# Sample attention's value products: every second key column, the sliding window and the new tokens as two tiles of 64 by 128 in place of four of 32 by 64

## The chip, the cores and the metric

The kernel runs on one core of a Trainium2 chip. The metric is the device time of one execution in microseconds (us). The engines of the core are TensorE (PE in the profile; its weight loads are PEld), VectorE (DVE), ScalarE (ACT), GpSimd (POOL) and SyncE (SP); the last two issue most of the data transfers. Each engine runs its own instructions in order and waits for the others by semaphores.

## The reference

One step of a decoder layer for a prompt of 512 tokens and for a sample group of 8 sequences with 8 new tokens each, on top of 2048 cached tokens a sequence. Only the sample group's attention matters here. Each sequence has two attention branches of 8 heads: "fox" (with forgetting) and "NSA" (three parts: selected blocks of keys, a sliding window of 512 keys, compressed keys). Both have 8 query heads, four to each of two key/value heads (groups) of 64 channels.

```python
def fox_attend(q, cq, q_pos, k, v, ck, k_pos):
    s = jnp.einsum('btgrd,bsgd->bgrts', q, k).astype(jnp.float32) * HEAD_DIM ** -0.5
    bias = jnp.moveaxis(cq, 1, -1)[..., :, None] - jnp.moveaxis(ck, 1, -1)[..., None, :]
    p = masked_softmax(s + bias, k_pos[None, :] <= q_pos[:, None])
    return jnp.einsum('bgrts,bsgd->btgrd', p.astype(v.dtype), v)

    # nsa_attend, its three products with values, g the group, r the head in it
    o_c = jnp.einsum('bgrtn,bngd->btgrd', p_c.astype(vc.dtype), vc)
    o_s = jnp.einsum('bgrtjs,bgtjsd->btgrd', p_s.astype(vsel.dtype), vsel)
    o_w = jnp.einsum('bgrtw,bwgd->btgrd', p_w.astype(vw.dtype), vw)
    return gates[..., 0:1] * o_c + gates[..., 1:2] * o_s + gates[..., 2:3] * o_w
```

For one sequence, one branch and one group there are 4 heads x 8 tokens = 32 query rows, and the values of that group have 64 channels. So a product with values is, for each group, weights (keys by 32) against values (keys by 64). Everything here is in f32.

## The kernel before

The sample attention is the method `sample_attention`. Its loop has a step for each of the 8 sequences `b`. The 2048 cached keys lie on 128 partitions in 16 columns `c` (`fr` for fox, `sr` for NSA; three such rooms are loaded in turn, `room` is the third), keys in the first 128 channels of a column, values in the last 128, both groups side by side. The 128 softmax rows are 2 branches x 2 groups x 32.

In a step, TensorE does the scores `ss` (`sequence_scores`, in four PSUM banks), the scores against the new tokens `sn`, then products with the values of the sequence before (`values(b - 1, ...)`). Meanwhile VectorE adds the biases into `S` (tile `zF`) and takes maxima, and ScalarE exponentiates in two halves. TensorE then transposes the weights (`turn_weights`: `spn`, then `sp` in four groups of four columns), ScalarE copies them to `T` (`spT` and `zK`), and TensorE does the first columns of `values(b, ...)` ahead of the next `ss`. The number of columns done where is: in even steps 12 of the sequence before and 8 of this one; in odd steps 8 and 4; the last sequence has its 16 at the end. Even steps also have the window's scores `sw`, odd steps the window's values (`window_values`, for two sequences at once) and `pair_sums` (`accS`), which picks out the results and adds them up. TensorE's instructions of the whole stage are chained in the order in which the code writes them (`link`); VectorE's and ScalarE's order is a scheduler's, within the bounds that `issue_after` sets.

The value products go into one PSUM bank, `so`. A key column is four products with 32 weight columns each (`quarters`):

```python
        for x in range(4):
            self.mm(self.sob[32 * x:32 * x + 32, col:col + 64], T[:, 32 * x:32 * x + 32],
                    values[x // 2][:, 64 * (x % 2):64 * (x % 2) + 64], start, stop)
```

Row quarter `x` of the bank belongs to branch `x // 2` and group `x % 2`. The new tokens' product (`TN`, 64 keys), the window's four columns (`TW`, 128 keys each), its new tokens (`TWn`) and the compressed keys (`pcT`, 127 keys) go the same way. `sequence_end` and `window_end` scale the results into `OA` and `OAw` on VectorE, and `sums` multiplies them by selection matrices into `accS`.

Of the kernel before, what the change touches and what calls it, by code (L numbers as in the profile page):

```python
# [6 lines left out]
F32 = mybir.dt.float32  # L7
# [4 lines left out]
OP = mybir.AluOpType  # L12
AX = mybir.AxisListType

P = 128
# [30 lines left out]
class Step:  # L46
# [55 lines left out]
    def ts(self, out, a, s1, s2, op0, op1=None, **kw):  # L102
        if op1 is None:
            self.last_ts = self.nc.vector.tensor_scalar(out, a, s1, s2, op0=op0, **kw).ins
        else:
            self.last_ts = self.nc.vector.tensor_scalar(out, a, s1, s2, op0=op0, op1=op1, **kw).ins
# [1513 lines left out]
    def sample_attention(self, sp, ctx):  # L1620

        t = lambda name, shape, dt=F32: sp.tile(shape, dt, name=name)
# [5 lines left out]
        self.T = [t(f"spT{i}", [P, 4, P]) for i in range(2)] + [  # L1628
            flat[1][:, 512 * i:512 * i + 512].rearrange("p (j n) -> p j n", j=4) for i in range(2)]
        self.sel, self.selW = [t(f"sel{g}", [P, 64]) for g in range(2)], [[t(f"selW{o}{g}", [P, 64]) for g in range(2)] for o in range(2)]  # L1630
        self.SN, self.OA, self.OAw = [[t(f"{n}{x}", [P, 64]) for x in range(2)] for n in ("sN", "OA", "OAw")]
        maps = [t(f"map{x}", [P, n]) for x, n in enumerate((2, 2, 2, 4))]
        pw = self.pool("spw", ctx)
        self.D3.append(pw.tile([P, 16, 32], F32, name="D3b"))
        pw.tile([P, 224], F32, name="edge")
        w1 = pw.tile([P, 4, 256], F32, name="wr1")
        self.CT = pw.tile([P, 512], F32R, name="CT")
        self.wrt = [pw.tile([P, 4, 256], F32, name="wr0"), w1]
# [26 lines left out]
        for b in range(NB):  # L1665
            n, odd = b // 2, b % 2
# [100 lines left out]
            self.cp(self.oT[:, 4 * a:4 * a + 4, SEQ:NT].rearrange("p r (b t) -> p r b t", t=8), av[:, a])  # L1767

    def pair_sums(self, n):
        w = self.OAw[n % 2]  # L1770
        for o in range(2):
            self.sums(2 * n + o, self.sel, self.OA[o], True)
            self.sums(2 * n + o, self.selW[o], w, False)

    def sample_maps(self, maps):

        jj = self.OA[0]
        self.iota(jj, [[1, 64]])
        col, up, gm, tmp = maps
        ts = self.ts  # L1780
        ts(up[:, 1:2], self.prow, 64.0, None, OP.is_ge)
        ts(up[:, 0:1], up[:, 1:2], -1.0, 1.0, OP.mult, OP.add)
        ts(col[:, 1:2], self.p31, 32.0, None, OP.add)
        self.stt(col[:, 0:1], up[:, 1:2], 32.0, self.p31, OP.mult, OP.add)
        self.cp(gm[:, 1:2], self.g_row)
        ts(gm[:, 0:1], self.g_row, -1.0, 1.0, OP.mult, OP.add)
        for g in range(2):
            ts(self.sel[g], jj, col[:, 0:1], gm[:, g:g + 1], OP.is_equal, OP.mult)
            for o in range(2):
                t = tmp[:, 2 * g + o:2 * g + o + 1]  # L1790
                self.tt(t, up[:, o:o + 1], gm[:, g:g + 1], OP.mult)
                ts(self.selW[o][g], jj, col[:, 1:2], t, OP.is_equal, OP.mult)
# [70 lines left out]
    def turn_weights(self, b):  # L1863
# [5 lines left out]
        for i in range(4):  # L1869
# [2 lines left out]
                self.tr(tb[:, P * j:P * j + P], self.S[:, 4 * i + j].rearrange("p q s -> p (q s)"))  # L1872
            self.last_weights = self.act(self.T[i], tb.rearrange("p (j n) -> p j n", j=4)).ins

    def quarters(self, col, T, values, start, stop):


        for x in range(4):
            self.mm(self.sob[32 * x:32 * x + 32, col:col + 64], T[:, 32 * x:32 * x + 32],
                    values[x // 2][:, 64 * (x % 2):64 * (x % 2) + 64], start, stop)  # L1880

    def values(self, b, part):
        col = 128 * (b % 2)
        fr, sr = self.rows[b]
        for i in part:
            T = self.T[i]
            for j in range(4):
                c = 4 * i + j
                self.quarters(col, T[:, j], (fr[:, c, P:256], sr[:, c, P:256]), c == 0, False)
        if part[-1] == 3:  # L1890
            self.quarters(col, self.TN, (self.vnew[:, 0, :], self.vnew[:, 1, :]), False, True)

    def sequence_end(self, b):

        mx, dn, nm = self.stat.pop(b)
        d = self.small.tile([P, 1], F32, tag="sd", name=f"sd{b}")
        self.nc.vector.tensor_reduce(d, dn, axis=AX.X, op=OP.add)
        self.nc.vector.reciprocal(d, d)
        col = 128 * (b % 2)
        self.ts(self.OA[b % 2], self.sob[:, col:col + 64], d, self.GA[:, b:b + 1], OP.mult, OP.mult)  # L1900
        self.last_end = self.last_ts

    def sums(self, b, sel, OA, first):

        for g in range(2):
            self.mm(self.acc[64 * g:64 * g + 64, 64 * b:64 * b + 64], OA, sel[g], first, not first)

    def window_keys(self, b):
        tb = self.trb(f"wk{b}")
# [33 lines left out]
        self.values(NB - 2, range(2, 4))  # L1943

    def window_values(self, i):
        col = 256 + 128 * (i % 2)
        wr = [self.wr.pop(2 * i + o) for o in range(2)]
        for j in range(4):
            self.quarters(col, self.TW[:, j], [w[:, j, P:256] for w in wr], j == 0, False)
        self.quarters(col, self.TWn, [self.vnew[:, 2, :]] * 2, False, True)  # L1950
        self.quarters(col + 64, self.pcT[:127, i], [self.vc[:127, 2 * i + o] for o in range(2)], True, True)

    def window_end(self, i):
        st, col = self.wst.pop(i), 256 + 128 * (i % 2)
        self.nc.vector.reciprocal(st[:, 3:4], st[:, 3:4])
        w = self.OAw[i % 2]
        self.ts(w, self.sob[:, col:col + 64], st[:, 3:4], self.GB[:, 1, i:i + 1], OP.mult, OP.mult)
        self.last_end = self.stt(w, self.sob[:, col + 64:col + 128], self.GB[:, 0, i:i + 1], w, OP.mult, OP.add).ins

    def mix_open(self):  # L1960

# [777 lines left out]
```

## Time and profile before

| | |
|---|---|
| median of 3 runs | 1146.51 us (1145.56 to 1148.76) |
| profiled execution | 1145.33 us, its span 1143.6 us |
| granted TensorE clock, mean | 0.992 |
| TensorE matmuls in the program | 9089 |
| matmuls into `so` | 1280, from 437.0 to 535.4 us |
| TensorE idle just before them, waiting for "issue" | 16.4 us, 18 times (loads and matmuls) |

A row of a timeline gives start, duration, engine, line, operation, tiles (out<-in) and shapes: "128*32 128x64" is a stationary operand of 128 partitions by 32 columns against a moving operand of 128 by 64. An f32 product is two matmul rows. Line 77 is the helper that all matmuls go through, so tiles tell them apart. A row of a stage has, in order, its length, the busy time (and instructions) of PE, PEld, DVE, ACT and POOL, the granted clock, the busy share of the transfer engines and GB/s. In the chain of waits, "issue" is time in which an engine waited for nothing that the profile shows.

### The profile page before, as it was taken

The numbers are of one execution on the slowest core, as the hardware profiler recorded it, in microseconds if no ns is written. First come the engines' busy times: TensorE is split into PE (matmuls) and PEld (weight loads), VectorE is DVE, ScalarE is ACT, GpSimd is POOL, SyncE is SP. The second block draws the span as 40 slices with busy tenths as digits, with TensorE's granted clock in tenths as the row PEclk, the third lists the DMA queues.
The fourth block names the chain that finished last, engine by engine and source line by source line (L and its number), as shares of the span: only waits on it lengthen the run. The fifth ranks groups of instructions, "written<-read, shape, count | busy, mean of one in ns | idle before, by whom it ended". The sixth has DMA issues, their size and how long they took to land.

```text
span 1143.6 us, 24614 instructions
## 1 busy us (share of the span) xinstructions
PE 1086.8 (95%) x9089; PEld 937.3 (82%) x9089; DVE 820.2 (72%) x2011; ACT 544.2 (48%) x1146; POOL 229.8 (20%) x319
## 2 busy tenths in 40 slices
PE   3999999999999997889999999999999999999998
PEld 3887789988666654556999999998988989899896
DVE  5988665675787867677977757669657657475668
ACT  3466653444777754457644434473413424143230
POOL 7540000001211414441000000012312122221202
PEclk9999999999999998999999999999999999999999
DMA  8998594764786799996543273351313224132132
GB/s 199 292 270 235 195 278 150 244 220 136 250 276 196 214 271 318 329 353 198 128 111 99 68 222 101 96 170 49 111 38 111 76 73 147 38 111 74 56 120 83
DMA packets 169049, 191.75 MB, mean 168 GB/s; under 512 B 17849, under 2 KB 147330, under 8 KB 166754
## 3 DMA queue, kind: packets, MB, share of 16 engines
q1 hardware_dynamic: 154818, 152.05, 44.8%
q0 software_dynamic: 11936, 37.10, 9.9%
q8 instruction: 71, 1.16, 0.4%
q10 hardware_dynamic: 2176, 1.05, 0.4%
q14 instruction: 48, 0.39, 0.1%
HBM read 179.89 MB, written 31.16 MB: 185 GB/s over the span
## 4 chain that ended last, share of the span: by engine, by line
PE 74%; DVE 10%; DMA 6%; ACT 4%; issue 3%; SPq 2%; POOL 1%; DVEq 0%; ACTq 0%; POOLq 0%
PE dn L77 16%; PE hid L77 5%; PE z L77 5%; PE br L77 4%; PE wo L77 4%; PE upv L77 3%; PE upx L77 3%; PE ss L77 3%; PE mg L77 2%; DMA winr<-in_w_in 2%; SPq L155 2%; PE so L77 2%; PE mgv L77 2%; PE mgx L77 2%; PE upz L77 2%
## 5 line engine op out<-in xcount | busy, mean ns | idle before, releaser
L100 DVE TENSOR_TENSOR acc<-acc,dn 128x512 f32<-128x512 f32 x66 | 44.5, 684 | 55.9 <-PE dn L77 55.9
L77 PE MATMUL hid<-xh,w1hlk 128*128 128x256 f32 (+1 forms) x192 | 46.7, 336 | 15.5 <-ACT xh L112 15.5
L77 PE MATMUL z<-winh,h2r 128*128 128x264 f32 (+1 forms) x288 | 57.3, 288 | 2.5 <-ACT adw L112 2.5
L77 PE MATMUL z<-winh,h 128*128 128x264 f32 (+1 forms) x288 | 55.9, 284 | 0.0
L112 ACT ACTIVATE xh<-cpg 128x512 fp32r<-128x512 f32 x64 | 37.4, 623 | 36.2 <-PE hid L77 20.5
L112 ACT ACTIVATE u<-c 128x512 fp32r<-128x512 f32 x64 | 24.1, 434 | 59.9 <-PE dn L77 45.3
L77 PE MATMUL hid<-xh,w1hlv 128*128 128x256 f32 (+1 forms) x192 | 48.1, 342 | 4.2 <-ACT w1hlv L112 2.9
L2403 POOL TENSOR_TENSOR wur<-wur 128x512 f32<-128x512 f32 x12 | 19.8, 1648 | 150.9 <-DVE wu1l L131 55.5
L131 DVE TENSOR_TENSOR xl<-cpg,xh 128x512 fp32r<-128x512 f32 x64 | 42.3, 682 | 10.1 <-ACT xh L112 10.1
L77 PEld LDWEIGHTS z<-winh,h2r 128*128 128x128 f32 x288 | 45.6, 190 | 3.8 <-ACT adw L112 2.7
L77 PEld LDWEIGHTS hid<-xh,w1hlk 128*128 128x128 f32 x192 | 32.6, 197 | 19.4 <-ACT xh L112 15.7
L77 PEld LDWEIGHTS z<-winh,h 128*128 128x128 f32 x288 | 45.8, 190 | 0.0
L470 DVE STREAM_TRANSPOSE cpg<-cpg 128x1024 f32<-128x1024 f32 (+1 forms) x36 | 39.2, 1109 | 8.8 <-DMA cpg<-in_cache_nsa_kv 8.8
L77 PE MATMUL z<-winl,h 128*128 128x264 f32 (+1 forms) x160 | 44.5, 284 | 0.5 <-DVE winl L131 0.5
L77 PE MATMUL z<-winl,h2r 128*128 128x264 f32 (+1 forms) x160 | 44.4, 284 | 0.0
L155 POOL DMA_DIRECT2D cpg<-in_cache_nsa_kv x72 | 37.7, 525 | 27.4 <-issue 13.7
L77 PEld LDWEIGHTS hid<-xh,w1hlv 128*128 128x128 f32 x192 | 33.7, 203 | 8.5 <-ACT w1hlv L112 3.1
L77 PE MATMUL br<-oL,wbh 128*128 128x288 f32 x128 | 37.7, 295 | 0.0
L77 PE MATMUL br<-oH,wbl 128*128 128x288 f32 x128 | 37.7, 294 | 0.0
L77 PE MATMUL br<-oH,wbh 128*128 128x288 f32 x128 | 37.7, 294 | 0.0
L1828 DVE CUSTOM_DVE_ANT_1 zF<-ss,scr 128x512 f32<-128x512 f32 x32 | 20.2, 687 | 20.2 <-PE ss L77 20.2
L131 DVE TENSOR_TENSOR winl<-winr,winh 128x1056 fp32r<-128x1056 f32 (+1 forms) x16 | 19.6, 1233 | 19.4 <-ACT winh L112 19.3
(926 smaller groups left out, 3604.3 us busy)
## 6 DMA issues: line engine op xcount, KB each, us to landing
adw<-in_w_ada SPq DMA_DIRECT2D x16, 1024.0 KB
foxD<-in_cache_fox_kv SPq DMA_DIRECT2D x128, 128.0 KB
wur<-in_w_up SPq DMA_DIRECT2D x32, 512.0 KB
wdr<-in_w_down SPq DMA_DIRECT2D x32, 512.0 KB
wada<-in_w_ada SPq DMA_DIRECT2D x8, 1024.0 KB
sr<-in_cache_nsa_kv SPq DMA_DIRECT2D x64, 128.0 KB
cpg<-in_cache_nsa_kv POOLq DMA_DIRECT2D x56, 128.0 KB, 6.0
cpg<-in_cache_nsa_kv SPq DMA_DIRECT2D x56, 128.0 KB
```

The costliest lines, as they stand in the source:

```text
L77: ins = self.nc.tensor.matmul(out, a, b, start=start, stop=stop, skip_group_check=True)
L100: self.nc.vector.tensor_tensor(out, a, b, op=op)
L112: return self.nc.scalar.activation(out, in_, f, **kw)
L131: self.splits.append((eng or self.nc.vector).tensor_tensor(l, x, h.bitcast(F32), op=OP.subtract).ins)
L155: self.issued[eng] = getattr(self.nc, eng).dma_start(out, in_).ins
L470: self.flipped = self.nc.vector.transpose(v, v).ins
L1828: self.nc.vector.tensor_tensor_reduce(self.S[:, :, q, :], pbs[q].rearrange("p (c s) -> p c s", s=32), self.ramp[:, None, 32 * (q % 2):32 * ...
L2403: gp(a12, a12, a11, op=OP.subtract)
```

## The change

`values` sends every second column (j even) and the new tokens to a new method `halves`, and so does `window_values` for all its products. A half is one branch: 64 weight columns (both groups) against the 128 value channels of both groups. Of the 64 by 128 result the two diagonal blocks of 32 by 64 (group with its own group) are wanted, the other two are not. Quarters now write their group's columns of the same 128, so that both kinds add into the same places; `OA` and `OAw` become 128 wide, and `sums` takes from them the 64 columns of its group. To make room, `OAw` has one buffer in place of two, the window has one set of 256 columns in place of two sets of 128, and an unused tile shrinks.

```diff
+    def halves(self, col, T, values, start, stop):
+
+        for o in range(2):
+            half = slice(64 * o, 64 * o + 64)
+            self.mm(self.sob[half, col:col + P], T[:, half], values[o], start, stop)
+
     def quarters(self, col, T, values, start, stop):
         for x in range(4):
-            self.mm(self.sob[32 * x:32 * x + 32, col:col + 64], T[:, 32 * x:32 * x + 32],
-                    values[x // 2][:, 64 * (x % 2):64 * (x % 2) + 64], start, stop)
+            c = 64 * (x % 2)
+            self.mm(self.sob[32 * x:32 * x + 32, col + c:col + c + 64], T[:, 32 * x:32 * x + 32], values[x // 2][:, c:c + 64], start, stop)
...
                 c = 4 * i + j
-                self.quarters(col, T[:, j], (fr[:, c, P:256], sr[:, c, P:256]), c == 0, False)
+                (self.quarters if j % 2 else self.halves)(col, T[:, j], (fr[:, c, P:256], sr[:, c, P:256]), c == 0, False)
         if part[-1] == 3:
-            self.quarters(col, self.TN, (self.vnew[:, 0, :], self.vnew[:, 1, :]), False, True)
+            self.halves(col, self.TN, (self.vnew[:, 0, :], self.vnew[:, 1, :]), False, True)
...
-        self.ts(self.OA[b % 2], self.sob[:, col:col + 64], d, self.GA[:, b:b + 1], OP.mult, OP.mult)
+        self.ts(self.OA[b % 2], self.sob[:, col:col + P], d, self.GA[:, b:b + 1], OP.mult, OP.mult)
...
         for g in range(2):
-            self.mm(self.acc[64 * g:64 * g + 64, 64 * b:64 * b + 64], OA, sel[g], first, not first)
+            self.mm(self.acc[64 * g:64 * g + 64, 64 * b:64 * b + 64], OA[:, 64 * g:64 * g + 64], sel[g], first, not first)
...
-        col = 256 + 128 * (i % 2)
+        col = 256
         wr = [self.wr.pop(2 * i + o) for o in range(2)]
         for j in range(4):
-            self.quarters(col, self.TW[:, j], [w[:, j, P:256] for w in wr], j == 0, False)
-        self.quarters(col, self.TWn, [self.vnew[:, 2, :]] * 2, False, True)
-        self.quarters(col + 64, self.pcT[:127, i], [self.vc[:127, 2 * i + o] for o in range(2)], True, True)
+            self.halves(col, self.TW[:, j], [w[:, j, P:256] for w in wr], j == 0, False)
+        self.halves(col, self.TWn, [self.vnew[:, 2, :]] * 2, False, True)
+        self.halves(col + P, self.pcT[:127, i], [self.vc[:127, 2 * i + o] for o in range(2)], True, True)
```

The order of the instructions shows it at three places. First TensorE, the last columns of the first block of sequence 0 (`so` from the weights `spT`) and the window's scores `sw` behind them, ahead of the next sequence's `ss`; before:

```order
L77 MATMUL so<-fr_6090,spT_6382 32x64 x2
L77 MATMUL so<-sr_5697,spT_6382 32x64 x2
L77 MATMUL sw_6711<-wkt_6408,bdN 64x512
L77 MATMUL sw_6711<-wkt_6409,bdN 64x512
L77 MATMUL ss_6737<-fr_6379,scr 32x512
```

and after, the last two columns:

```order
L77 MATMUL so<-fr_6090,spT_6382 64x128
L77 MATMUL so<-sr_5697,spT_6382 64x128
L77 MATMUL so<-fr_6090,spT_6382 32x64 x2
L77 MATMUL so<-sr_5697,spT_6382 32x64 x2
L77 MATMUL sw_6702<-wkt_6407,bdN 64x512
L77 MATMUL sw_6702<-wkt_6408,bdN 64x512
L77 MATMUL ss_6728<-fr_6379,scr 32x512
```

The product of a column with fox and NSA values is four instructions in a quarter column, two in a half column, and the two kinds alternate. Second TensorE, the end of a window's values (`wr` its cached values, `vnew` the new ones, `vc` the compressed ones) and the first sums; before:

```order
L77 MATMUL so<-wr_6406,scr 32x64 x2
L77 MATMUL so<-wr_6404,scr 32x64 x2
L77 MATMUL so<-vnew,TWn 32x64 x4
L77 MATMUL so<-vc,pers 32x64 x4
L77 MATMUL accS<-sel_6383,OA_6391 64x64
```

and after:

```order
L77 MATMUL so<-wr_6405,scr 64x128
L77 MATMUL so<-wr_6403,scr 64x128
L77 MATMUL so<-vnew,TWn 64x128 x2
L77 MATMUL so<-vc,pers 64x128 x2
L77 MATMUL accS<-sel_6383,OA_6391 64x64
```

Here all are halves, and the sums that follow are tiles of 64 columns too. Third VectorE in step 0, between the window's score biases and the biases of sequence 1 (`sel`, `selW` and `map` are the selection matrices made once, `sr` the keys of sequence 1); before:

```order
L106 TENSOR_SCALAR selW_6387<-OA_6391,map_6395,map_6398 128x64
L106 TENSOR_SCALAR selW_6385<-OA_6391,map_6395,map_6398 128x64
L100 TENSOR_TENSOR map_6398<-map_6396,map_6397 128x1
L106 TENSOR_SCALAR selW_6388<-OA_6391,map_6395,map_6398 128x64
L1955 RECIPROCAL swst_6595<-swst_6595 128x1
L1809 STREAM_TRANSPOSE sr_6380<-sr_6380 128x4x128
```

and after:

```order
L106 TENSOR_SCALAR selW_6387<-OA_6391,map_6394,map_6397 128x64
L1810 STREAM_TRANSPOSE sr_6380<-sr_6380 128x4x128
L106 TENSOR_SCALAR selW_6385<-OA_6391,map_6394,map_6397 128x64
L100 TENSOR_TENSOR map_6397<-map_6395,map_6396 128x1
L106 TENSOR_SCALAR selW_6388<-OA_6391,map_6394,map_6397 128x64
L1961 RECIPROCAL swst_6594<-swst_6594 128x1
```

The transpose of the last keys of sequence 1 stands four instructions earlier.

More of the change, by code (lines that the diff above doesn't have):

```diff
@@ L1630, in sample_attention @@
         self.sel, self.selW = [t(f"sel{g}", [P, 64]) for g in range(2)], [[t(f"selW{o}{g}", [P, 64]) for g in range(2)] for o in range(2)]
-        self.SN, self.OA, self.OAw = [[t(f"{n}{x}", [P, 64]) for x in range(2)] for n in ("sN", "OA", "OAw")]
+        self.SN = [t(f"sN{x}", [P, 64]) for x in range(2)]
+        self.OA, self.OAw = [t(f"OA{x}", [P, P]) for x in range(2)], t("OAw", [P, P])
         maps = [t(f"map{x}", [P, n]) for x, n in enumerate((2, 2, 2, 4))]
@@ L1634, in sample_attention @@
         self.D3.append(pw.tile([P, 16, 32], F32, name="D3b"))
-        pw.tile([P, 224], F32, name="edge")
+        pw.tile([P, 96], F32, name="edge")
         w1 = pw.tile([P, 4, 256], F32, name="wr1")
@@ L1769, in pair_sums @@
     def pair_sums(self, n):
-        w = self.OAw[n % 2]
+        w = self.OAw
         for o in range(2):
@@ L1775, in sample_maps @@
     def sample_maps(self, maps):
-        jj = self.OA[0]
+        jj = self.OA[0][:, 0:64]
         self.iota(jj, [[1, 64]])
@@ L1945, in window_values @@
     def window_values(self, i):
-        col = 256 + 128 * (i % 2)
+        col = 256
         wr = [self.wr.pop(2 * i + o) for o in range(2)]
         for j in range(4):
-            self.quarters(col, self.TW[:, j], [w[:, j, P:256] for w in wr], j == 0, False)
-        self.quarters(col, self.TWn, [self.vnew[:, 2, :]] * 2, False, True)
-        self.quarters(col + 64, self.pcT[:127, i], [self.vc[:127, 2 * i + o] for o in range(2)], True, True)
+            self.halves(col, self.TW[:, j], [w[:, j, P:256] for w in wr], j == 0, False)
+        self.halves(col, self.TWn, [self.vnew[:, 2, :]] * 2, False, True)
+        self.halves(col + P, self.pcT[:127, i], [self.vc[:127, 2 * i + o] for o in range(2)], True, True)
     def window_end(self, i):
-        st, col = self.wst.pop(i), 256 + 128 * (i % 2)
+        st, col = self.wst.pop(i), 256
         self.nc.vector.reciprocal(st[:, 3:4], st[:, 3:4])
-        w = self.OAw[i % 2]
-        self.ts(w, self.sob[:, col:col + 64], st[:, 3:4], self.GB[:, 1, i:i + 1], OP.mult, OP.mult)
-        self.last_end = self.stt(w, self.sob[:, col + 64:col + 128], self.GB[:, 0, i:i + 1], w, OP.mult, OP.add).ins
+        w = self.OAw
+        self.ts(w, self.sob[:, col:col + P], st[:, 3:4], self.GB[:, 1, i:i + 1], OP.mult, OP.mult)
+        self.last_end = self.stt(w, self.sob[:, col + P:col + 2 * P], self.GB[:, 0, i:i + 1], w, OP.mult, OP.add).ins
     def mix_open(self):
```

## The prediction

> **What bounds the kernel now.** I read the page first, then the stages, then the chain of waits and TensorE's rows where the changed tile `so` is written. The page and two stages:
>
> ```profile
> span 1143.6 us, 24614 instructions
> PE 1086.8 (95%) x9089; PEld 937.3 (82%) x9089; DVE 820.2 (72%) x2011; ACT 544.2 (48%) x1146; POOL 229.8 (20%) x319
> 437.00:536.00 99.00, 83.65 (x2027) 53.68 (x2027) 67.51 (x213) 51.33 (x113) 35.97 (x70) 0.97 0.88 298
> 536.00:740.00 204.00, 203.83 (x1595) 202.50 (x1594) 156.39 (x329) 96.55 (x176) 6.71 (x12) 1.00 0.42 120
> ```
>
> The change touches only 437 to 536 us, the eight sequences of the sample. There TensorE (first pair of numbers) idles 15 of 99 us; behind it TensorE is full (203.83 of 204.00), so a delay or gain at 536 us reaches the end undiminished. What the changed lines cost, and what TensorE waits for:
>
> ```profile
> L77 PE MATMUL so<-fr,spT x192: 216/219/317, 437.0 to 534.2; 128*32 128x64 f32 x192
> PE so L77 <- issue: 7.2, 6, 2.2
> PE sp L83 <- issue: 2.0, 1, 2.0
> PE ss L77 <- issue: 0.8, 1, 0.8
> ```
>
> The longest waits are "issue", 10.0 us, waits for nothing the profile shows. Where do they fall? Take one stage between two of them, and the queue that carries instructions over 425 to 545 us:
>
> ```profile
> 488.93:494.68 5.75, 4.98 (x128) 3.69 (x128) 5.75 (x13) 5.45 (x12) 4.01 (x8) 1.00 1.03 342
> q8 instruction: 17, 0.28, 0.9%
> ```
>
> 128 matmuls and 128 weight loads: 256 instructions between one wait's end and the next. Counted in the trace, all nine such waits end at instruction 193 of a block of 256. 0.28 MB in 17 packets is 16.5 KB each, and the page's 9089 + 9089 instructions over its 71 packets are 256 a packet. So these are waits for the next block of instructions, fetched while the DMA engines are full (share 1.03). Start to start the nine gaps sum to 12 us: a block was used up before the next arrived.
>
> **The change part by part.** On TensorE, of every four key columns two keep four tiles of 32 by 64 ("quarters") and two get two of 64 by 128 ("halves"), in turn. What each costs, from TensorE's rows in order of time:
>
> ```profile
> 459.04 0.23 PE L77 MATMUL so<-fr,zK 128*32 128x64 f32 x2
> ...
> 459.26 0.23 PE L77 MATMUL so<-fr,zK 128*32 128x64 f32 x2
> ...
> 461.77 0.25 PE L77 MATMUL so<-fr,zK 128*32 128x64 f32 x2 [2.24 <-issue]
> ...
> 461.85 0.22 PE L77 MATMUL so<-fr,zK 128*32 128x64 f32 x2
> ...
> 461.97 0.22 PE L77 MATMUL so<-fr,zK 128*32 128x64 f32 x1
> ...
> 462.13 0.32 PE L77 MATMUL so<-vnew,TN 64*32 64x64 f32 x8
> ```
>
> An f32 product is two passes; four tiles run side by side, and four passes take 459.26 - 459.04 = 0.22 us, 0.055 a pass, 0.11 a column. The first pass after a break takes 0.08 (461.77 to 461.85), its weight load being uncovered. Where the tile shape changes, the last pass takes 0.16 (461.97 to 462.13): the array runs empty first. Halves are not in this trace; their nearest rows are the two 64-column tiles of `accS` and a 128-wide transpose ahead of `so`:
>
> ```profile
> 478.49 0.32 PE L77 MATMUL so<-vc,pers 127*32 127x64 f32 x8
> 478.73 0.34 PE L77 MATMUL accS<-sel,OA 128*64 128x64 f32 x4
> 478.90 0.29 PE L77 MATMUL accS<-selW,OAw 128*64 128x64 f32 x4
> 479.02 0.29 PE L77 MATMUL accS<-sel,OA 128*64 128x64 f32 x4
> ...
> 447.12 0.30 PE L83 MATMUL spwn<-identF,scr 128*64 128x128 f32 x1
> 447.35 0.25 PE L77 MATMUL so<-fr,zK 128*32 128x64 f32 x2
> ```
>
> Two regular passes of 64 moving columns take 0.12 (478.90 to 479.02), the first two 0.17: 0.05 of load uncovered. 32 to 64 columns empties the array too: 0.24 from 478.49 to 478.73 for a first pass and a last (0.08 + 0.16). A pass of 128 moving columns takes 0.109 (16 transposes in 1.75 us, row 491.46 below), and one followed by another tile shape 0.23, of which 0.05 is load: 0.18 to 0.21.
>
> So a half column between two quarters costs 0.05 + 0.11 + 0.21 = 0.37, and a quarter column between two halves 0.08 + 0.16 = 0.24: **0.61 a pair, where a pair cost 0.22**. If the array did not empty between the two shapes, it would be 0.22 + 0.11 = 0.33. I take 0.61, since every change of shape in the rows above, both ways, shows the emptying. [...]
>
> A block of 12 columns thus gains 2.2 us, of 8 columns 1.4, of 4 columns 0.65, the last of 16 columns 3.0 (0.39 a pair, less the 0.1 by which the old block ended in a change anyway). The 8-row token product (`TN`) goes from 0.24 to 0.37, eight times. A window's four columns, all halves without a change between them, go from 0.5 to 1.0, its `TWn` gains 0.1; the compressed product is followed by `accS` in the same shape and gains nothing. In all 3 x 2.2 + 8 x 1.4 + 3 x 0.65 + 3.0 + 8 x 0.13 + 4 x 0.6 = **26 us more on TensorE**.
>
> Against it, 384 matmuls and 384 loads fewer in this stage, three blocks of 256. A block's time rises from about 6.5 us to 8 or 9, more than nearly all the fetch times seen (intervals of 5.6 to 8.4 us where TensorE waited). I let the nine waits go and keep 0.5 us.
>
> Neither sum lies wholly on the path. From the end of `ss` TensorE needs nothing for 5.75 us but has `so` of the sequence before to do, while VectorE and ScalarE make the softmax. An even step shows both parts:
>
> ```profile
> 481.98 3.82 PE ss L77 x67
> ...
> 487.53 0.69 PE so L77 x38
> 488.21 0.71 issue
> 488.93 1.30 PE so L77 x66
> 490.22 1.01 PE sw L77 x4
> ...
> 491.46 1.75 PE sp L83 x16
> 493.21 0.69 PE so L77 x40
> 493.90 0.77 issue
> 494.68 0.54 PE so L77 x24
> 495.22 3.40 PE ss L77 x68
> 490.42 1.13 ACT L112 ACTIVATE zF<-zF,ss 128x1024 f32<-128x1024 f32 x1
> ```
>
> The last row is ScalarE's: the second half's exponentials end at 491.55, 5.75 us after `ss` (485.80), and TensorE comes to `sp` at 491.46. There is no slack left: 12 columns and token, 2.0 now plus the wait of 0.7, become 4.1, and 8 columns, 1.2 plus 0.8, become 2.5: 1.9 us longer, less 0.3 that `ss` now waits at its start. Rows of an odd step (5), of the last, and of one stage inside step 2:
>
> ```profile
> 500.16 1.31 issue
> 501.47 2.13 PE so L77 x97
> ...
> 505.97 1.97 issue
> ...
> 521.41 3.34 PE ss L77 x63
> 524.75 0.82 issue
> ...
> 533.43 2.17 PE so L77 x136
> 464.00:465.00 1.00, 1.00 (x7) 1.00 (x6) 1.00 (x3) 0.92 (x2) 0.35 (x1) 0.50 1.08 354
> ```
>
> Step 5: 8 and 4 columns, token and window add 2.2; both waits (3.3) go: -1.1. Done so for each step, from one `ss` to the next: step 2, 3.6 more against its wait of 2.2 (2.24 above) and some 1.6 for the half clock that followed it (0.50 in the last row, while `sp` and `wk` ran): -0.2; step 3, +0.2; step 4, +1.6; step 5, -1.1; step 6 (no wait in it) 3.8 more, of which 1.3 fills waits for exponentials and for the next `ss`: +2.5; step 7, 16 columns at its open end (3.0), 1.4, 0.1 and 0.6 before it, less 0.8 of wait and 0.3 of cover: +4.0. Together +7.0. Step 0 has 8 columns ahead of a VectorE chain that sets the next `ss`: +1.2, less 0.6 since VectorE's transpose now stands ahead of three mask operations. Step 1: +0.9. With the 0.5 kept, **+9 us**.
>
> The wider normalisations on VectorE (16 or so by 64 elements, 0.07 us each) lie under TensorE's work; the loads that POOL issues when `so` frees a room come later by as much as TensorE does. The shared `OAw` and window columns are rewritten a whole step after their last reader.
>
> The profiled execution took 1145.3 us, 1.2 under the runs' median of 1146.5. On it the sum gives 1154.3, on the median 1155.5; I say 1155.
>
> **The rivals.** (1) *No emptying between the two column widths*, the one that makes it faster: 0.33 a pair. Then 12 columns are 2.0, inside the softmax's 5.75; steps fall to what VectorE and ScalarE need, and stage 437 to 536 ends 4.1 us earlier in steps 2 to 7, later by 0.7 in 0 and 1: 1143. For it: the tiles stand on the same columns and the rows at 128 partitions. Against: 478.49 to 478.73 is exactly this change, and it emptied. It decides at about 0.41 a pair (3.4 of the 12.4 us between the two cases, from 0.33). (2) *The issue waits stay*, moved to other blocks: the columns' cost without the gain. Without the waits the old steps 2 to 7 would end 5.1 us earlier, so 1155.5 + 5.1 = 1161. Against: fewer instructions in more time. [...] (3) *The softmax covers more*: the even steps' extra is hidden as step 2's, and only step 7's 4.0 less some of the waits is left: within 3 us, 1148.
>
> **How the numbers follow.** Forecast 0.62 (1151 to 1160 by itself: the drain at 0.18 or 0.21 and waits of 0 to 4 us left); rival 1, 0.12; rival 2, 0.13; rival 3, 0.13. A measurement of this kernel tells about 0.3%, 3.4 us. Faster: most of rival 1 and some of 3: 0.12. Same: 0.14. Slower: 0.74. The range leaves out a tenth at each end: 1145 to 1163.
>
> **What would show it.** Matmuls fall to 8705. Right: `so` rows of 64 columns with 0.2 us from a half's second pass to the next quarter and 0.16 back; "issue" below 3 us; the stage longer by 9 us, most in steps 4, 6 and 7. Wrong: a pair of columns at 0.33 (rival 1), or waits of 1 to 2 us still every 256 instructions (rival 2).

## The result, and the profile after

| | before | the change |
|---|---|---|
| median | 1147.44 us (7 runs) | 1155.25 us (7 runs) |
| ratio | | 1.0065, 95% interval 1.0036 to 1.0094 |
| the same once more, beside another set of runs of before | 1145.76 us (23 runs) | 1155.71 us (6 runs), 1.0102 (1.0073 to 1.0130) |
| profiled execution, its span | 1145.33, 1143.6 us | 1155.25, 1153.6 us |

The change makes the kernel slower, by 8 us in one set of runs and by 10 in the other; 9 was forecast (1155, range 1145 to 1163). The change's page (engines; the queue that carries instructions, with packets and MB):

```profile
span 1153.6 us, 23844 instructions
PE 1109.7 (96%) x8705; PEld 945.3 (82%) x8705; DVE 824.3 (71%) x2011; ACT 545.3 (47%) x1146; POOL 229.0 (20%) x319
q8 instruction: 68, 1.11, 0.4%
```

Two stages of it, the second taken 10 us later, since the sample's stage now ends about that much later:

```profile
437.00:536.00 99.00, 95.01 (x1499) 54.97 (x1495) 67.82 (x210) 48.35 (x108) 35.44 (x69) 0.98 0.86 289
546.00:750.00 204.00, 203.83 (x1590) 202.61 (x1590) 153.63 (x323) 91.19 (x165) 4.90 (x9) 1.00 0.39 111
```

TensorE has 384 matmuls fewer, the queue that carries instructions has 68 packets in place of 71, and TensorE is busy 22.9 us longer (19.1 in a second profile, see 1 below). In the sample's stage its idle time fell from 15 to 4 of 99 us; the stage behind it is as full as before. So the idle time was filled and more than filled. The view of TensorE's waits in this stage (what waited, for what: us, times, longest):

```profile
PE ss L77 <- DVE sr L1810: 2.0, 1, 2.0
PE so L77 <- ACT zK L112: 1.2, 1, 1.2
PE sn L77 <- ACT wkt L112: 0.5, 2, 0.3
...
```

No "issue" is left of the 10 us. A new wait of 1.2 us stands ahead of a product with values; it comes back below. One pair of columns in TensorE's rows by time: the last passes of a quarter column, a half column, a quarter column and the start of the next half.

```profile
458.31 0.23 PE L77 MATMUL so<-fr,spT 128*32 128x64 f32 x2
...
458.47 0.32 PE L77 MATMUL so<-fr,spT 128*64 128x128 f32 x1
...
458.63 0.27 PE L77 MATMUL so<-fr,spT 128*64 128x128 f32 x1
...
458.84 0.25 PE L77 MATMUL so<-fr,spT 128*32 128x64 f32 x2
...
458.92 0.23 PE L77 MATMUL so<-fr,spT 128*32 128x64 f32 x2
...
459.09 0.32 PE L77 MATMUL so<-fr,zK 128*64 128x128 f32 x1
```

From the first pass of a half (458.47) to that of the next (459.09) the pair takes 0.62 us: 0.16 from a quarter's last pass into the half, 0.16 for the half's first pass, 0.21 from its second into the quarter, 0.08 for the quarter's first. 0.61 was forecast.

Where the time went, from the start of one step's `ss` to the next (the last, to the first `mg`), in us. The last column is the change's second profile:

| step | before | the change | moved | forecast | the change again |
|---|---|---|---|---|---|
| 0 and 1 | 32.83 | 34.82 | +2.0 | +1.5 | 34.89 |
| 2 | 14.81 | 14.84 | 0.0 | -0.2 | 14.80 |
| 3 | 12.81 | 12.59 | -0.2 | +0.2 | 12.59 |
| 4 | 13.24 | 14.45 | +1.2 | +1.6 | 14.49 |
| 5 | 13.74 | 12.63 | -1.1 | -1.1 | 12.59 |
| 6 | 12.52 | 14.45 | +1.9 | +2.5 | 14.49 |
| 7 | 14.12 | 21.51 | +7.4 | +4.0 | 18.82 |

Step 7 alone is far off. The stage starts up to 8 us earlier or later from one profile to the next, whatever the kernel (first `ss` between 418 and 426 us); so below kernels are compared by these steps and by their timed ratios, not by spans. That the first profile took just the 1155 that was forecast is luck: its step 7 holds time that the forecast did not have (see 1).

### The profile page after: what moved, and what is told of

It is laid out like the page before. It is cut to its first block, busy times and chain, and to the rows that moved or that the text cites. A ratio compares the mean times of both kernels' runs of the same rounds, so it can differ in the third digit from the quotient of the medians.

```text
span 1153.6 us, 23844 instructions
## 1 busy us (share of the span) xinstructions
PE 1109.7 (96%) x8705; PEld 945.3 (82%) x8705; DVE 824.3 (71%) x2011; ACT 545.3 (47%) x1146; POOL 229.0 (20%) x319
## 4 chain that ended last, share of the span: by engine, by line
PE 81%; DMA 6%; DVE 5%; SPq 3%; ACT 2%; issue 2%; POOL 0%; ACTq 0%; POOLq 0%; DVEq 0%
PE dn L77 18%; PE z L77 9%; PE br L77 4%; PE wo L77 4%; PE so L77 4%; PE up L77 4%; PE upx L77 3%; PE upv L77 3%; DMA cpg<-in_cache_nsa_kv 3%; SPq L155 3%; PE ss L77 2%; PE mg L77 2%; PE hid L77 2%; PE mgv L77 2%; PE mgx L77 2%; PE upy L77 2%
## 5 line engine op out<-in xcount | busy, mean ns | idle before, releaser
L77 PE MATMUL hid<-xh,w1hlk 128*128 128x256 f32 (+1 forms) x192 | 46.6, 335 | 15.2 <-ACT xh L112 15.2
L131 DVE TENSOR_TENSOR xl<-cpg,xh 128x512 fp32r<-128x512 f32 x64 | 42.3, 683 | 10.2 <-ACT xh L112 10.1
L112 ACT ACTIVATE wu1h<-wur 128x512 fp32r<-128x512 f32 (+1 forms) x21 | 13.5, 651 | 40.9 <-PE upv L77 24.6
```

What stands on the lines that cost most here:

```text
L77: ins = self.nc.tensor.matmul(out, a, b, start=start, stop=stop, skip_group_check=True)
L112: return self.nc.scalar.activation(out, in_, f, **kw)
L131: self.splits.append((eng or self.nc.vector).tensor_tensor(l, x, h.bitcast(F32), op=OP.subtract).ins)
```

## Experiments

The ratio stands beside the median of the runs of before that were made with it: 1145.22 us (first four), 1145.76 (the change again, split halves, left out, light loads), 1146.03 (to the fifth, behind, behind with window), 1144.53 (the last). Apart from the change each kernel has one profile; those of left out, light loads and behind are of the longest execution of their kernel, so a wait that stands there need not be in the median.

**1. The change once more.** No edit.

> The change once more, unaltered, to see whether the 10 us of half TensorE clock at the end of its stage (537.5 to 547.7 us in its profile) belong to it. Theory (they follow from the wait of 1.2 us for ScalarE there): they are in this profile too, and the time is 1155. Rival (they fall by the history of the execution, as the dips of 3 us elsewhere do): step 7 takes some 17 us in place of 21.5 and the profiled execution 1151.

Measured: 1155.71 us, ratio 1.0102 (1.0073 to 1.0130); the profiled execution took 1151.35 us. The same stretch of both as a stage, the first profile of the change, then this one:

```profile
537.00:547.50 10.50, 10.50 (x110) 6.72 (x109) 6.21 (x10) 6.46 (x12) 1.80 (x3) 0.52 0.77 245
```

```profile
537.00:547.50 10.50, 10.50 (x147) 8.25 (x142) 9.07 (x14) 7.84 (x14) 1.80 (x3) 1.00 0.79 270
```

The granted clock is the third number from the right: 0.52 against 1.00. In the first profile 110 matmuls went through in this time, in the second 147. Step 7 falls from 21.51 to 18.82 us, and the 16 `mg` products behind it from 3.72 to 2.33. So about 4 us of the first profile are a half clock that this change does not need to have; the rival was right. Steps 0 to 6 agree within 0.1 us in both profiles. The second profile is of the shortest of its six executions.

**2. Halves grouped.** Halves in the first two of each four columns, quarters in the last two: the same instructions, half the changes of shape.

```diff
-                (self.quarters if j % 2 else self.halves)(col, T[:, j], ...
+                (self.quarters if j // 2 else self.halves)(col, T[:, j], ...
```

> The change, but of each four key columns the first two are halves and the last two quarters: the same 8705 matmuls, half as many changes of tile shape. Theory (each change of shape empties the array): four columns cost 0.59 + 0.35 = 0.94 us in place of 2 x 0.618 = 1.24, 9.6 us less TensorE work over the stage, about two thirds of it on the path: 1149 us, with no waits of 1 to 2 us back at the ends of instruction blocks. Rival (the halves themselves are dear, wherever they stand): nothing changes, 1155.

Measured: 1145.18 us, ratio 1.0004 (0.9980 to 1.0027). Pieces of the chain of waits, of the change (second profile) and of this kernel: 4 columns, 12 with the token product, 8 columns, and the last 16 with theirs.

```profile
507.21 1.24 PE so L77 x24
...
513.56 3.93 PE so L77 x76
...
520.47 2.47 PE so L77 x48
...
536.38 5.38 PE so L77 x100
```

```profile
479.85 0.95 PE so L77 x24
...
510.95 3.06 PE so L77 x76
...
517.00 1.90 PE so L77 x48
...
531.80 4.23 PE so L77 x100
```

The same number of the same matmuls in 1.90 us in place of 2.47, in 0.95 in place of 1.24: it is the changes of shape that cost, 0.29 us for each change there and back that is taken away. 0.94 us was worked out for four columns. Steps 2 to 7 are 6.5 us shorter than the change's (second profile). No gap at a boundary of 256 instructions came back. I had 1149: the 6 us on the path were right, and steps 0 and 1 are 1.8 us shorter as well, which I had not worked out.

**3. All halves.** No change of shape within a block, 8449 matmuls.

```diff
-                (self.quarters if j % 2 else self.halves)(col, T[:, j], ...
+                self.halves(col, T[:, j], ...
```

> Every key column as two tiles of 64 by 128, so no change of shape inside a block of columns, and 256 matmuls fewer than in the change. Theory (cost is the change of shape): a pair of columns at 4 x 0.109 = 0.44 us in place of 0.618, 12 columns 2.7 us in place of 3.7, together 11.6 us less TensorE work, about two thirds on the path: 1147 us. Rival (the wide tiles are dear by themselves): a pair stays at 0.6 or more, 1155 or later.

Measured: 1142.78 us, ratio 0.9976 (0.9952 to 1.0001). Second passes of three columns on end, TensorE's rows by time:

```profile
454.30 0.27 PE L77 MATMUL so<-fr,spT 128*64 128x128 f32 x1
...
454.52 0.27 PE L77 MATMUL so<-fr,spT 128*64 128x128 f32 x1
...
454.74 0.27 PE L77 MATMUL so<-fr,spT 128*64 128x128 f32 x1
```

Two passes, a column, in 0.22 us; two columns 0.44, as worked out, against 0.62 for a mixed pair. A column of halves alone is dearer than one of quarters (0.11) but cheaper than the mixture. The ratio is at the edge of what can be told from before, and about 0.01 below the change's. I had 1147: steps 2 to 7 are 7.5 us shorter than the change's (second profile), as expected, and steps 0 and 1 by some 3 more.

**4. Quarters in the last sequence.**

```diff
-                (self.quarters if j % 2 else self.halves)(col, T[:, j], ...
+                (self.quarters if j % 2 or b == NB - 1 else self.halves)(col, T[:, j], ...
```

> The change, but the 16 key columns of the last sequence, which stand at the open end of the stage, are all quarters. Theory (the end of the stage is slow because its 16 columns run at half clock after TensorE waited for ScalarE, and because they alternate): the 16 columns take 2 to 3.5 us in place of 7.4, so 4 to 6 us less: 1150. Rival (what was lost at the end would be caught up behind it, since the next stage waits for other work): 1154 to 1155.

Measured: 1149.94 us, ratio 1.0040 (1.0016 to 1.0063). Its step 7 takes 15.80 us, with the full clock, against 18.82 in the change's profile with the full clock. The last 16 columns with their token product, from its chain of waits:

```profile
538.78 2.36 PE so L77 x132
```

5.38 us became 2.36, and the 3.0 come off the end: nothing behind the stage catches them up. The time of the change that the half clock adds in its first profile is not part of this difference, so my 4 to 6 was too much.

**5. Halves in the window and the new tokens only.** All key columns are quarters, 8961 matmuls.

```diff
-                (self.quarters if j % 2 else self.halves)(col, T[:, j], ...
+                self.quarters(col, T[:, j], ...
```

> Only the window's products and the new tokens are halves; all key columns are quarters (8961 matmuls). Theory (waits for the next block of instructions return with the short blocks, at instruction 193 of 256): most of the nine waits, 8 to 12 us from start to start, are back, TensorE works 3.4 us longer than before the change, about two thirds on the path: 1149 us. Rival (the nine waits come from something other than the number of instructions per time): the waits stay away or fall at other places, and the time is 1143 or less.

Measured: 1146.43 us, ratio 1.0003 (0.9979 to 1.0026). Six waits are back, and in the trace each ends at instruction 193 of 256, as the nine did before; start to start they take 6.6 us, of which the profile counts the longer ones as "issue", like this one of TensorE's rows:

```profile
478.54 0.44 PE L77 MATMUL so<-vc,pers 127*64 127x128 f32 x4 [1.04 <-issue]
```

They fall on other instructions than before (scores, the token product, the compressed product), but at the same place in their blocks. I had 8 to 12 us and 1149; that the window's longer products already take some of the waits is likely, but no run shows it by itself.

**6. Split halves.** Each half as two instructions of 64 moving columns: 9089 matmuls as before the change, with its changes of shape. (Its result leaves out the first key column for one group; the time is that of the same instructions.)

```diff
-            self.mm(self.sob[half, col:col + P], T[:, half], values[o], start, stop)
+            for c in range(0, P, 64):
+                self.mm(self.sob[half, col + c:col + c + 64], T[:, half], values[o][:, c:c + 64], start, stop)
```

> The change, but each half is done in two instructions of 64 moving columns in place of one of 128: 9089 matmuls as before the change, the same changes of tile shape. Theory (the waits for instruction blocks go by fewer instructions): they return, some 5 us on the path, beside the same emptying of the array: 1160 us. Rival (they go because a block of 256 takes longer, whatever makes it longer, the emptying included): blocks last 7.5 to 8 us, few waits return, and the time is 1155 to 1157.

Measured: 1157.88 us, ratio 1.0096 (1.0059 to 1.0133), not to be told from the change's 1.0102. TensorE's waits in the stage:

```profile
PE so L77 <- DVE OAw L109: 1.6, 1, 1.6
PE ss L77 <- DVE sr L1810: 1.3, 1, 1.3
PE so L77 <- issue: 1.2, 3, 0.4
```

Four gaps at block boundaries are left, 2.0 us from start to start, of the 12 us before. So most of the waits go with as many instructions as before: a longer time per block is enough (6.5 us in place of 5.2, counted as under "Why they go" below), and here the changed tiles make up that time. What the fewer instructions are worth beside it is small: steps 2 to 6 are 3.1 us longer here than in the change (second profile), 2.0 of them these gaps, and the timed ratios do not tell the two kernels apart.

**7. Instructions left out.** The kernel before; in three of each four key columns two of the four tiles are left out.

```diff
-        for x in range(4):
+        for x in some:
...
-                self.quarters(col, T[:, j], (...), c == 0, False)
+                self.quarters(col, T[:, j], (...), c == 0, False, (0, 3) if j else range(4))
```

> The kernel before, with two of the four tiles of 32 by 64 left out in every key column but the first of each four (part of the products with values is not computed): 8705 matmuls as in the change, no change of tile shape, each pass as long as before. It prices the instruction saving alone. Theory: most of the nine waits are gone, 5 us on the path: 1140 us, so the emptying of the array costs the change some 13 us on the path. Rival (the waits are hidden behind the softmax anyway): 1145.

Measured: 1141.34 us, ratio 0.9957 (0.9937 to 0.9976). The gaps at block boundaries shrink from 12 to 2.0 us (three), and steps 2 to 7 together from 81.2 to 76.5 us. The forecast had 5.1 us for this. The rest of the waits' 12 us could not be had, since other waits end later; TensorE's in the stage:

```profile
PE ss L77 <- issue: 2.8, 3, 1.3
PE ss L77 <- DVE sr L1809: 2.6, 1, 2.6
PE sp L83 <- ACT zF L112: 2.5, 3, 0.8
PE spn L83 <- ACT sN L112: 1.7, 2, 1.5
```

TensorE now comes early to the transposes and waits 2.5 us for ScalarE's exponentials (`zF`), and at the start of `ss` it waits three times, up to 1.3 us, for something that the profile does not name; none of these three is at a block's boundary. Against the change in the same set of runs the difference is 14.4 us: that is about what the changed tiles cost on the path when most of the waits for instructions are gone on both sides. It includes the change's 2.0 us in steps 0 and 1 and its new wait of 1.2, and left out still has 2.0 of gaps.

**8. Fewer transfers.** The kernel before; the fox rows of sequences 5 to 7 are not loaded.

```diff
+            if b < 5:
                 self.sample_fox(b, i, "sync" if i % 2 else "gpsimd")
```

> The kernel before, with the fox rows of sequences 5, 6 and 7 not loaded (their fox scores and values use old rows): the same instructions on TensorE, about half of the transfers from some 475 us on. Theory (instruction blocks come late because the transfer engines are full): the waits ahead of 475 us stay, the five behind it shrink from 7 us to under 2, and the time falls by about 3 to 1142 us. Rival (a block takes that long to fetch however free the engines are): they stay as they are, 1145.

Measured: 1142.05 us, ratio 0.9967 (0.9948 to 0.9986). Two stages of before (the transfer engines' share is the number before the last):

```profile
500.00:506.00 6.00, 4.66 (x139) 3.74 (x128) 5.93 (x16) 4.26 (x12) 2.05 (x5) 1.00 1.05 370
506.00:512.00 6.00, 4.06 (x98) 1.88 (x98) 1.26 (x4) 1.66 (x4) 2.28 (x5) 1.00 1.04 403
```

The same two and a later one of this kernel (its stage starts 5 us later, so the same time shows work that lies 5 us earlier in the kernel):

```profile
500.00:506.00 6.00, 6.00 (x197) 3.69 (x165) 4.17 (x18) 2.35 (x7) 2.20 (x6) 1.00 0.61 194
506.00:512.00 6.00, 5.05 (x106) 3.08 (x102) 4.80 (x10) 4.58 (x10) 2.64 (x5) 1.00 0.87 299
530.00:536.00 6.00, 4.97 (x133) 3.83 (x133) 2.42 (x7) 6.00 (x12) 1.59 (x3) 1.00 1.02 380
```

And one of its rows of TensorE by time:

```profile
538.37 0.25 PE L77 MATMUL so<-sr,zK 128*32 128x64 f32 x2 [2.91 <-issue]
```

The four waits of before between 488 and 508 us are gone, with the same instructions on TensorE, and the one ahead of them, at 477, fell from 2.0 to 0.3 us from start to start; there a block's packet now starts 0.7 to 3.1 us after the boundary ahead of it, where it started 3.2 to 4.9 us after it before. Of the three waits ahead of 475 us two stayed (2.7 and 0.5 us); that the third, of 0.65, is gone too, the lighter loads do not explain. One of 0.6 is left at 526. And one new wait of 3.1 us came in the last sequence, in a stretch where the transfers are still full (share 1.02): the kernel got there with its blocks cut at another point of the traffic. So fewer transfers took four waits away with the same instructions, and in these profiles a block came late mostly where the transfer engines were full: before, their share is 0.97 to 1.06 in the 3 to 5 us ahead of seven of the nine waits, 0.50 ahead of the first and 0.76 ahead of the last. Full engines are not enough: at 534.61 us, with 1.02 ahead of it, a boundary has no gap. The five waits from 488 us on were to shrink from 7 us to under 2; in this profile those that are left take 3.8, but it is of the longest of ten executions, and the median came out at the 1142 that I had.

**9. Four mixtures of whole blocks.** What the runs so far say for this kernel: no mixing of shapes within a block of columns (0.29 us for each change there and back, under 2), and the dear halves (0.22 us a column against 0.11) where they lie beside the softmax. "To the fifth": sequences 0 to 5 all halves, 6 and 7 all quarters. The line of the new tokens (`TN`) is changed in the same way in all four kernels and is not shown.

```diff
-                (self.quarters if j % 2 else self.halves)(col, T[:, j], ...
+                (self.halves if b < 6 else self.quarters)(col, T[:, j], ...
```

> Sequences 0 to 5 all halves (key columns and new tokens), sequences 6 and 7 all quarters, window as in the change; no change of shape inside a block. Theory (what all halves lose is the doubled stream where nothing covers it: step 6 and the open end in step 7): 8 columns of sequence 6 ahead of the last scores, 8 behind them and the last 16 at 0.11 us less each, 3 us less than with all halves, and no wait for instructions there: 1139.5 us. Rival (a wait of 1 to 3 us for an instruction block falls into 524 to 540 us, where the transfers are full): 1142.

Measured: 1140.30 us, ratio 0.9960 (0.9937 to 0.9983), as expected: its step 6 takes 12.97 and step 7 14.72 us, with all halves 13.79 and 15.63.

"Behind": halves only in blocks that follow the scores.

```diff
-                (self.quarters if j % 2 else self.halves)(col, T[:, j], ...
+                (self.halves if b < NB - 1 and part[0] else self.quarters)(col, T[:, j], ...
```

> Halves only in the blocks that follow the scores and lie beside the softmax (12 columns in even steps, 8 in odd ones, with the new tokens); quarters in the blocks between the turned weights and the next scores and in the last sequence; window as in the change. Theory (a stream that the softmax covers is free, and the longer block keeps the waits for instructions away): 44 columns ahead of the scores and 16 at the end at 0.11 us less than with all halves, 4 to 5 us of it on the path: 1138 us. Rival (the shorter blocks bring the waits back): 1142 or later.

Measured: 1143.80 us, ratio 0.9984 (0.9963 to 1.0005), not the 1138 that I expected. Step 5 takes 12.72 us where to the fifth has 11.80: a block of instructions comes 1.9 us late, at instruction 193, ahead of `sn`. Step 7 has the new wait of 1.2 us that the change has. Both are in its view of TensorE's waits:

```profile
PE sn L77 <- issue: 1.4, 1, 1.4
PE so L77 <- ACT zK L112: 1.2, 1, 1.2
```

"Behind, with window": the same, with quarters in all the window's products but for the first pair of sequences.

```diff
+        tiles = self.quarters if i else self.halves
-            self.halves(col, self.TW[:, j], ...
+            tiles(col, self.TW[:, j], ...
```

> The last but with quarters in the window's products too, except for the first pair of sequences. Theory (the window's products stand in the softmax's time of the odd steps and are mostly covered): within 1 us of the one with halves in the window, 1138. Rival (the window is on the path): 1.5 us less, 1136.5. If waits for instruction blocks return, 1140 or later.

Measured: 1139.49 us, ratio 0.9947 (0.9922 to 0.9972): below both the kernel before and the change. Its page:

```profile
span 1140.9 us, 23966 instructions
PE 1091.1 (96%) x8765; PEld 942.4 (83%) x8765; DVE 823.3 (72%) x2011; ACT 544.8 (48%) x1146; POOL 230.0 (20%) x319
```

And its waits in the stage. Neither of the two is among them; only a gap of 0.4 us is called "issue":

```profile
PE ss L77 <- DVE sr L1810: 2.6, 1, 2.6
PE wk L83 <- DMA wr<-in_state_win_kv: 1.0, 1, 1.0
...
PE ss L77 <- issue: 0.4, 1, 0.4
```

Whether the 4 us to "behind" are the window's shorter products or the two waits that happen not to be there, these runs do not part: its steps 5 and 7 are shorter by 1.4 each, which is about what the waits were, steps 2 to 4 and 6 within 0.3.

The last also takes halves for sequence 0's first columns, for the order of VectorE in step 0.

```diff
-                (self.halves if b < NB - 1 and part[0] else self.quarters)(...
+                (self.halves if b < NB - 1 and (part[0] or b == 0) else self.quarters)(...
```

> The last kernel, but sequence 0 takes halves in its first 8 columns too (ahead of the scores of step 1). That moves one of VectorE's transposes of keys ahead of the last mask operations, the order that the kernel with all halves has there. Theory (steps 0 and 1 are set by that order: 31.9 us with all halves, 32.9 with the last kernel): 1 us less, 1138.5. Rival (0.9 us more TensorE work in step 0 is on the path): 1140.4.

Measured: 1141.79 us, ratio 0.9979 (0.9960 to 0.9999). Steps 0 and 1 take 31.72 us against 32.90, as the theory had it, but a wait of 1.1 us for instructions is back in step 5 and steps 4 to 7 are longer by 1.4 together. The intervals of the two overlap; it is no gain over the one before.

## Why the prediction was right, and where not

**The waits are for blocks of instructions, and they go.** Right, and now by experiment: with fewer transfers the four waits in that stretch vanish (8), with other tiles they fall on other instructions at the same place of the block (5). The trace of before shows it too: each of the nine waits ends 1.3 to 1.6 us after a packet of the instruction queue has landed. Not every boundary has such a wait: of the sixteen between 437 and 536 us seven have no gap. At the nine with a gap a packet of the queue had started 3.2 to 5.9 us after the boundary ahead; of the seven without, at five it had started 1.1 to 2.7 us after it, at the two others 3.8 and 6.8 us after it, in blocks that lasted 6.4 and 15.2 us. The forecast kept 0.5 us of these waits; none was left.

**Why they go.** The prediction gave two reasons, 384 matmuls and loads fewer and a longer time per block. Split halves (6) take the first away, left out (7) the dearer passes; in each only 2.0 of the 12 us are there. So either is enough for most of it, and both come to one quantity, the time that a block lasts by itself. Counted between 452 and 531 us, from one boundary to the next with the gaps taken off, it is 5.2 us before, 6.0 in window only, 6.5 in split halves, 6.9 in left out and 7.7 in the change; the gaps in the same stretch are 11.5, 6.5, 2.0, some 2 and 0 us. The prediction had 8 to 9 us a block for the change.

**A pair at 0.61 us.** Right: 0.62, and its parts as taken from the rows of `accS` and the transposes. Grouping (2) and all halves (3) show that it is the change of shape. Eight columns of before (step 2) in its chain of waits:

```profile
467.13 1.03 PE so L77 x64
```

They went from 1.03 to the 2.47 us shown under 2, forecast +1.4; the last sixteen with token from 2.17 to 5.38, forecast +3.1. What the prediction calls the emptying of the array is a time in the rows: before, no weight load and no pass starts on TensorE from the quarter's last pass at 461.98 us to the token product's load at 462.13, 0.15 us, where passes of one shape start 0.055 us apart and the next pass's loads start beside them. What the array does in that time no run shows. Rival 1, a pair at 0.33 us, is out. No run shows the time it would have given; left out, which also has 8705 matmuls without the changes of shape, but computes less, has 1141 us, where 1143 was given.

**Steps 2 to 6.** The softmax covers as much as was worked out: the sum of their forecasts was +3.0, they took +1.8. Step 5 came out by two slips: the prediction's own terms for its columns, token and window make 2.8 (1.4, 0.65, 0.13 and 0.6), not 2.2, and they took 2.7 more; its two gaps, counted as 3.3, are 3.8 from start to start. Rival 3, more cover, is out: steps 4 and 6 lengthen by 1.2 and 1.9. Rival 2, waits that stay, is out by the view of waits.

**Step 7 was mis-sized,** +4.0 against +4.7 at full clock and +7.4 in the first profile. What failed is the term that let TensorE go from `sp` straight on to the 16 columns. It waits 1.2 us there. The view of waits names ScalarE's copy `zK`; VectorE's rows by time say otherwise. Of before:

```profile
530.22 0.34 DVE L106 TENSOR_SCALAR OAw<-so,swst,GB 128x64 f32<-128x64 f32 x1
...
531.72 0.28 DVE L109 SCALAR_TENSOR_TENSOR OAw<-so,GB,OAw 128x64 f32<-128x64 f32 x1
...
532.59 1.23 DVE L131 TENSOR_TENSOR wml<-wmr,wmh 128x1024 fp32r<-128x1024 f32 x1 [0.53 <-ACT wmh L112]
```

Of the change (second profile), with the row of TensorE that waits:

```profile
534.30 1.22 DVE L131 TENSOR_TENSOR wml<-wmr,wmh 128x1024 fp32r<-128x1024 f32 x1 [0.28 <-ACT wmh L112]
535.44 0.41 DVE L106 TENSOR_SCALAR OAw<-so,swst,GB 128x128 f32<-128x128 f32 x1
535.88 0.35 DVE L109 SCALAR_TENSOR_TENSOR OAw<-so,GB,OAw 128x128 f32<-128x128 f32 x1
...
536.38 0.29 PE L77 MATMUL so<-fr,spT 128*64 128x128 f32 x1 [1.24 <-ACT zK L112]
```

The window's normalisation (`OAw`), which reads the same bank `so`, stood ahead of VectorE's split of a weight (`wml`) before; in the change it stands behind it and ends at 536.23, 0.15 us before the product starts. The product needs the first copy into `spT`, not the last into `zK`, which ends at nearly the same time by chance. The semaphore instruction that stands just ahead of the product in TensorE's queue waits for VectorE's semaphore, which this `OAw` raises; in the change's first profile it does so at 536.47, the semaphore instruction ends at 536.55 and the product starts at 536.61. In split halves, where the copies are done earlier, the waits name `OAw` itself (1.6 us). In the fourteen profiles, the wait stands in all eight that have `OAw` behind `wml` (both of the change among them) and in none of the six that have it ahead. So the change reordered VectorE, though it does not touch `wml`; the prediction costed VectorE's wider normalisations at nothing, as lying under TensorE's work, and did not ask where they stand in the queue. Their lengths it had right (0.07 us more each, in the rows above). The 16 columns with token (+3.2) and the wait (+1.2) make 4.4 of the 4.7, so the rest of the step took 0.3, where about 1 was given.

**Steps 0 and 1.** +2.0 against +1.5. The kernels whose sequence 0 takes halves alone have 31.7 to 31.9 us there, 32.8 before: VectorE's order there, which the forecast counted at 0.6 us, changes with small edits. No run changes this order alone, so its price is not shown.

**The sum.** In the second profile, whose step 7 has the full clock, steps 0 and 1 to 7 moved by +2.1, 0.0, -0.2, +1.2, -1.2, +2.0 and +4.7, together +8.6; the forecast was +9 with 0.5 of waits kept. Two errors of about a microsecond, too much in steps 4 and 6 and too little in 7, cancel; that the sum came this close is in part luck.

## What to carry to other kernels

A tile shape that needs fewer instructions is worth having only if whole runs of instructions share it and its longer stream is covered: a half column took 0.22 us of TensorE where a quarter column took 0.11, and taken in turn each there and back cost another 0.29. In whole blocks, kept away from the open end of the stage, halves were faster than before (ratios 0.9960 and 0.9947 under 9). Where TensorE's waits all end at the same place of blocks of 256 instructions, as the nine did here at instruction 193, find what fills the transfer engines and how long a block lasts: lighter traffic took four of the waits away here, fewer instructions or longer ones each left 2.0 of the waits' 12 us, and in window only, light loads and behind other instructions were hit than before. After an edit, compare the order on the engines that it does not mean to touch: here 1.2 us came from a normalisation on VectorE that slipped behind another operation.

## What the hardware did that was not expected

TensorE's granted clock of 0.5 came for 10.2 us (537.5 to 547.7) in one profile of the change and for none of that time in the other, behind the same wait of 1.24 us. Split halves show it too (540 to 550 us, behind a wait of 1.6), light loads for some 3 us behind its wait of 2.9; five other kernels with a wait of 1.2 us there do not. The records of the granted clock say more. In each of the fourteen profiles the changes of the clock fall on a grid of 3.41 us, which lies at another time in each profile; a stretch of 0.5 in this stage lasts one, two or three of its windows (3.41, 6.83 or 10.24 us). The window just ahead of these three stretches leaves TensorE idle for 1.69 us (the change's first profile), 1.88 (split halves) and 2.28 (light loads). In the change's second profile and in the five others no window there has more than 1.68. In the profile of before and the first of the change, from end to end, nine windows at full clock were followed by one at half clock; they have 1.69 us of idle time or more, the other 640 at full clock at most 1.51. So the same code met half clock in one profile and not in the other, with 1.69 and 1.68 us of idle time in the window ahead. In the 10 us at half clock TensorE was busy all through (10.50 of 10.50 us in the stage under 1). Whether the idle time sets the half clock off, and what kept it for three windows, is open: no run here was made to tell.

Left out has the same number of matmuls as the change and was faster by 14.4 us. Over the kernels here the order by time follows neither the number of matmuls nor TensorE's busy time; the runs above point to the waits and the changes of shape.
